# Experts of a two-layer decoder: raw float32 weights held in the array in 64-column tiles, 88 slots of tokens moving

## The chip, the cores and the metric

The kernel runs on one core of one Trainium2 chip. The metric is the device time of one execution in microseconds. Times come from three timed runs and from one profiled execution; instruction times (start and length in us) are those of the profiled execution.

## The reference

512 tokens of 1024 features go through two residual layers. Layer 0 mixes tokens by an RWKV-7 recurrence and a stick-breaking attention, layer 1 by a gated linear recurrence; all of that stays as it is. Each layer ends in a mixture of 16 experts, of which every token uses two:

```python
def hier_moe(h, ...):               # h = rmsnorm(x, norm_ffn[layer]), 512 x 1024
    ...                             # dense_gate: 512 x 16, two entries of a row not zero
    for e in range(N_EXPERTS):
        hid = jax.nn.silu(hf @ exp_w_gate[e]) * (hf @ exp_w_up[e])
        y = y + dense_gate[:, e:e + 1] * (hid @ exp_w_down[e])
```

An expert has 1024 x 512 weights for gate, as many for up, and 512 x 1024 for down, 6 MB of float32; 16 experts in two layers are 192 MB that are read once.

## The kernel before

**Routing.** `route_tile` runs once per tile of 128 tokens when the mixer has finished that tile (X). POOL multiplies the tile by the norm's gain (L1159), ACT's queue stores it in DRAM as HD (L1160) and the tile itself as YD (L1161), TensorE computes the router's logits (L1174). `choose` and `route` find every token's two experts, its place among an expert's tokens and its gate. Each expert has 96 slots (SL). For an expert's slots, `slots` compares places with slot numbers on VectorE (`match`, L1225), multiplies the result with the tokens' rows, gates and 1/rms on TensorE (`rows_of`, L1291) and reduces them on VectorE (L1283), so that each slot has three values: row of its token, gate, 1/rms. POOL gathers the slots' rows from HD (L1295).

**An expert.** `across` turns the 96 x 1024 gathered rows feature-major by eight transposes (L1306) and splits them into two float32r parts, hi and lo, whose sum is the float32 value: ACT copies (L296), VectorE subtracts (L297). Weights are split in the same way by `chunk`, in twelve half-parts an expert, of which POOL subtracts three and VectorE nine. Tokens stand in the array (128 x 96), weights move 512 columns at a time, and three matmuls (hi hi, lo hi, hi lo) make one float32 product: 24 for gate, 24 for up (L1317 to L1319), 24 for down (L1344 to L1346). The results are token-major, 96 partitions. SiLU with 1/rms as its scale runs on ACT (L1323), VectorE multiplies with up (L1456), `turn` transposes the hidden values (L1330) and splits them. `down` of expert e - 1 comes after gate and up of expert e; its two halves leave PSUM on ACT and VectorE, times the gate, and POOL adds them to YD in DRAM (L1353). The last expert's rows are added on chip (L1496 to L1510), after X has been read back from YD (L1481).

**Weights.** SP's queue loads an expert in six parts of 1 MB (L1371), at most five under way at a time, into a ring of slots of 2048 columns each. Gate and up parts have four rows of 2 KB per partition, down parts two of 4 KB. In layer 0 16 parts are loaded ahead, in layer 1 17; from there on a part's load waits until a slot is free.

**Order.** A scheduler orders each engine's instructions. `behind` adds order constraints: splits of the first expert's weights come after its slots are known, and so on. The SBUF has two arenas, A of float32 and R of float32r (12288 columns), R holding the split parts during the experts, and a piece S that changes its type.

## Time and profile before

| | |
|---|---|
| three runs, median (lowest to highest) | 1262.41 us (1259.56 to 1267.37) |
| profiled execution, span | 1262.0 us |
| TensorE busy | 1186.4 us, 94% |
| VectorE busy | 1028.6 us, 82% |
| ACT busy | 797.2 us, 63% |
| POOL busy | 497.1 us, 39% |
| DMA moved | 279.67 MB |
| mean granted TensorE clock | 0.971 |

The span is that of the first to the last instruction of the profiled execution, and the profiled execution is one more than the three timed ones. The experts of layer 0 take from 419.67 to 714.4 us, those of layer 1 from 954.2 to 1249.5, together 590 us of the 1262. A line of a timeline has start, length, engine, source line, operation, output tile and input tile, shapes (partitions x elements) and a count; for a matmul `128*64 128x88` is stationary rows x columns, then the moving operand. Matmuls are pipelined, so one starts before the one ahead of it has ended; what a matmul costs is read from the distance of starts. A float32 matmul leaves two records.

### The profile page before, as it was taken

The page shows a single profiled execution, that of the slowest core. Times are in us where ns is not written, and L with a number is a line of the kernel's source. Part 1 is how long each engine was busy: PE and PEld are TensorE (multiplying, and loading weights), DVE is VectorE, ACT ScalarE, POOL GpSimd, SP SyncE. Part 2 cuts the span into 40 slices and gives each one's busy share as a digit, 9 for nine tenths or more (in the row PEclk, how much of TensorE's full clock was granted, in tenths as well). Part 3 has the DMA queues.
Part 4 walks back from the last instruction along what each step waited for, and adds up shares of the span by engine and source line. Part 5 has one row for each costly group of instructions (what it writes and reads, how often), then busy time and mean ns, then how long its engine had stood idle before and what let it go on. Part 6 is the DMA issues. An engine that isn't in the chain of part 4 may idle for free. (4 is left out here: it accounts for less than half of the span.)

```text
span 1262.0 us, 17252 instructions
## 1 busy us (share of the span) xinstructions
PE 1186.4 (94%) x6234; PEld 875.7 (69%) x6235; DVE 1028.6 (82%) x1290; ACT 797.2 (63%) x1059; POOL 497.1 (39%) x326
## 2 busy tenths in 40 slices
PE   6999998999998799999999899999978999999997
PEld 5767765877676577777776676677865777777764
DVE  5387899577775899999998665599658999999985
ACT  6534332387653588888888564575435888888882
POOL 8043200211012347666775301220123466767752
PEclk9999999899998799999999999999987999999998
DMA  6312221001876799999998622267587999999974
GB/s 167 84 50 67 67 67 34 27 18 49 291 266 238 247 333 366 362 365 358 357 361 275 162 61 73 61 199 248 192 294 237 329 365 362 364 356 354 366 242 147
DMA packets 153060, 279.67 MB, mean 222 GB/s; under 512 B 7366, under 2 KB 58247, under 8 KB 152967
## 3 DMA queue, kind: packets, MB, share of 16 engines
q1 hardware_dynamic: 142886, 248.64, 56.8%
q0 software_dynamic: 7776, 21.47, 7.7%
q10 hardware_dynamic: 2304, 8.39, 1.7%
q8 instruction: 51, 0.84, 0.3%
q14 instruction: 43, 0.34, 0.1%
HBM read 259.59 MB, written 23.07 MB: 224 GB/s over the span
## 5 line engine op out<-in xcount | busy, mean ns | idle before, releaser
L296 ACT ACTIVATE R<-A 128x1024 fp32r<-128x1024 f32 (+1 forms) x451 | 473.2, 1053 | 201.7 <-PE ps_pj L1318 68.3
L297 DVE TENSOR_TENSOR R<-A,R 128x1024 fp32r<-128x1024 f32 (+1 forms) x362 | 493.1, 1397 | 77.2 <-ACT R L296 72.9
L297 POOL TENSOR_TENSOR R<-A,R 128x1024 fp32r<-128x1024 f32 x89 | 258.1, 2900 | 221.6 <-ACT R L296 219.8
L1317 PE MATMUL ps_pj<-R 128*96 128x512 f32 x512 | 204.9, 400 | 0.0
L1318 PE MATMUL ps_pj<-R 128*96 128x512 f32 x512 | 202.9, 396 | 1.6 <-DVE R L297 1.6
L1319 PE MATMUL ps_pj<-R 128*96 128x512 f32 x512 | 203.9, 398 | 0.0
L324 PE MATMUL ps_pj<-R 128*128 128x512 f32 x296 | 121.1, 409 | 9.9 <-DVE A L709 9.2
L326 PE MATMUL ps_pj<-R 128*128 128x512 f32 x296 | 119.3, 403 | 3.5 <-DVE R L297 3.5
L325 PE MATMUL ps_pj<-R 128*128 128x512 f32 x296 | 121.4, 410 | 0.0
L1318 PEld LDWEIGHTS ps_pj<-R 128*96 128x96 f32 x512 | 83.6, 163 | 37.7 <-DVE R L297 2.7
L1344 PE MATMUL ps_at<-R 128*96 128x512 f32 x256 | 103.8, 407 | 5.1 <-ACT R L296 1.9
L1319 PEld LDWEIGHTS ps_pj<-R 128*96 128x96 f32 x512 | 83.2, 163 | 36.0
L1317 PEld LDWEIGHTS ps_pj<-R 128*96 128x96 f32 x512 | 83.6, 163 | 34.2 <-ACT R L296 0.5
L1346 PE MATMUL ps_at<-R 128*96 128x512 f32 x256 | 101.6, 397 | 0.0
L1345 PE MATMUL ps_at<-R 128*96 128x512 f32 x256 | 101.5, 396 | 0.0
L324 PEld LDWEIGHTS ps_pj<-R 128*128 128x128 f32 x296 | 56.2, 190 | 27.6 <-DVE A L709 11.1
L1159 POOL TENSOR_TENSOR A<-A 128x1024 f32<-128x1024 f32 x8 | 20.9, 2623 | 135.3 <-DVE A L858 87.5
L326 PEld LDWEIGHTS ps_pj<-R 128*128 128x128 f32 x296 | 56.4, 191 | 20.7 <-DVE R L297 5.6
L1353 POOL DMA_INDIRECT YD<-A x30 | 67.3, 2245 | 4.8 <-issue 2.3
L325 PEld LDWEIGHTS ps_pj<-R 128*128 128x128 f32 x296 | 56.2, 190 | 15.3 <-issue 4.5
L1225 DVE TENSOR_TENSOR A<-A 128x384 bf16<-128x384 f32 (+2 forms) x34 | 61.8, 1818 | 0.0
L1295 POOL DMA_INDIRECT A<-HD,A x32 | 40.6, 1268 | 47.4 <-DVE A L1256 16.9
(440 smaller groups left out, 2067.7 us busy)
## 6 DMA issues: line engine op xcount, KB each, us to landing
A<-in_exp_w_up_dram SPq DMA_DIRECT2D x61, 1024.0 KB
A<-in_exp_w_down_dram SPq DMA_DIRECT2D x61, 1024.0 KB
A<-in_exp_w_gate_dram SPq DMA_DIRECT2D x59, 1024.0 KB
A<-in_w_in_even_dram SPq DMA_DIRECT2D x27, 512.0 KB
A<-in_w_in_odd_dram SPq DMA_DIRECT2D x20, 512.0 KB
S<-in_exp_w_gate_dram SPq DMA_DIRECT2D x5, 1024.0 KB
A<-in_w_out_odd_dram SPq DMA_DIRECT2D x10, 512.0 KB
A<-in_x_dram SPq DMA_DIRECT2D x8, 512.0 KB
```

Source lines behind the costliest of these rows:

```text
L296: a = self.nc.scalar.activation(hi, src, AF.Copy)
L297: return a, (eng or self.nc.vector).tensor_tensor(lo, src, hi.bitcast(F32), OP.subtract)
L324: nc.tensor.matmul(p[0:n], hi[:, k], Hh[:, k], start=k == 0, stop=False)
L325: nc.tensor.matmul(p[0:n], hi[:, k], Hl[:, k], start=False, stop=False)
L326: nc.tensor.matmul(p[0:n], lo[:, k], Hh[:, k], start=False, stop=k == KD - 1)
L1317: self.nc.tensor.matmul(b, xh[:, k], hi, start=k == 0, stop=False)
L1318: self.nc.tensor.matmul(b, xl[:, k], hi, start=False, stop=False)
L1319: self.nc.tensor.matmul(b, xh[:, k], lo, start=False, stop=k == KD - 1)
L1344: nc.tensor.matmul(yb[n], hh[:, k], hi[:, cs], start=k == 0, stop=False)
L1345: nc.tensor.matmul(yb[n], hl[:, k], hi[:, cs], start=False, stop=False)
L1346: nc.tensor.matmul(yb[n], hh[:, k], lo[:, cs], start=False, stop=k == 3)
L1353: self.nc.gpsimd.indirect_dma_start(out=self.YD[l][:, :], out_offset=bass.IndirectOffsetOnAxis(ap=ix[0:SL], axis=0), in_=y.rearrange("p a ...
```

## The change

**Weights aren't split.** The raw float32 weights are the stationary operand, in tiles of 128 rows and 64 columns, and tokens move (88 columns). `product` issues for one tile of 128 features eight matmuls for gate or up and sixteen for down; two neighbouring ones go to the left and right half of the array and write partitions 0 to 63 and 64 to 127 of one bank. An expert has 192 such matmuls instead of 72, with float32 products. Results are feature-major, so that the hidden values need no `turn`; the output of down does: `leave` copies it out of PSUM (ACT one half, VectorE the other), `back` transposes it (eight transposes of 128 x 128 to 88 x 128) and scales it by the gate. `down` runs in its own expert, after the next expert's `across`; `back` comes after the next expert's gate.

**88 slots** in place of 96. HD holds normed rows: `route_tile` computes 1/rms first, ACT multiplies by it, POOL by the gain while it reorders the features (reading with a stride of eight), into one buffer `hn`. 1/rms leaves the slots, which have two values.

**Loads.** Gate and up are laid out with features p*8 + c*4 + k, so that a part is one row of 8 KB per partition. R becomes float32 during the experts and holds six more weight slots; one old slot goes. 21 parts are loaded ahead in layer 0. The order constraints of `behind` go.

```diff
-SL = 96
-POOL = ((1, 1), (3, 1), (5, 1))
+SL = 88
...
     def route_tile(self, t):
+        r = self.rstd(t, self.ss)
         h = self.scr.next()
-        nc.gpsimd.tensor_tensor(h.f(), self.X.f(NT, D)[:, t], self.gn.f(), OP.mult)
+        nc.scalar.activation(h.f(), self.X.f(NT, D)[:, t], AF.Copy, scale=r)
+        n = self.hn.next()
+        turned = lambda a: a.rearrange("p (q k) -> p k q", k=KD)
+        nc.gpsimd.tensor_tensor(n.f(KD, 128), turned(h.f()), turned(self.gn.f()), OP.mult)
+        h = n
...
+    def leave(self, g, out, p):
+        pv = p[:, 0:4 * SL].rearrange("p (k t) -> p k t", k=4)
+        if g:
+            self.nc.vector.tensor_copy(out, pv)
+        else:
+            self.nc.scalar.activation(out, pv, AF.Copy)
+
+    def product(self, banks, raw, x, k, last):
+        for b, p in enumerate(banks):
+            pv = p[:, 0:4 * SL].rearrange("p (j n) -> p j n", j=4)
+            for j in range(4):
+                for s in range(2):
+                    q, c = slice(s * 64, s * 64 + 64), (b * 4 + j) * 128 + s * 64
+                    self.nc.tensor.matmul(pv[q, j], raw[:, c:c + 64], x, start=k == 0 and j == 0, stop=last, skip_group_check=True)
+
+    def half(self, w, x, chunk):
+        b = self.bank("pj")
+        for c in range(2):
+            raw = chunk(w * 2 + c)
+            for j in range(4):
+                k = c * 4 + j
+                self.product([b], raw[:, j], x[:, k], k, k == KD - 1)
+        return b[:, 0:4 * SL].rearrange("p (j n) -> p j n", j=4)
...
+    def back(self, yt, y=None, g=None):
+        nc = self.nc
+        yb = [self.bank("rw")[0:SL] for _ in range(2)]
+        for n in range(2):
+            for j in range(4):
+                nc.tensor.transpose(yb[n][:, j * 128:j * 128 + 128], yt[:, n * 4 + j], self.ident)
+        if y is None:
+            return yb
+        nc.scalar.activation(y[:, 0], yb[0], AF.Copy, scale=g)
+        nc.vector.tensor_scalar(y[:, 1], yb[1], g, None, OP.mult)
...
-            src = I["exp_w_gate" if i < 2 else "exp_w_up"][l].rearrange("e (c k p) n -> (e c) p k n", c=2, p=128)
-            return src, e * 2 + i % 2, (4, 512)
+            src = I["exp_w_gate" if i < 2 else "exp_w_up"][l].rearrange("e (p c k) n -> e c p (k n)", c=2, p=128)
+            return src[:, i % 2], (4, 512)
...
+        rr.drop(self.rat, RCOLS)
+        self.rat = ar.take(self.swap("R", F32), RCOLS)
         self.prefetch(l, 5, False)
         self.prefetch(l, 1, False, XB[0:1])
         if l:
             self.prefetch(l, 1, False, [self.more])
         self.prefetch(l, 1, False, XB[1:2])
+        self.prefetch(l, 6, False, [Buf(ar, self.rat.at + i * 2048, 2048) for i in range(6)])
         self.route(l)
...
-        self.prefetch(l, 1, False)
...
+        for e in range(NE):
             part = lambda i, e=e: self.chunk(l, e, i)
+            h = hr.next().f(4, SL)
+            self.front(h, self.half(0, x, part))
+            if e:
+                rest(e - 1)
             if e < NE - 2:
                 self.slots(e + 2)
                 fetch(e + 2)
-            if e:
-                h = self.turn(prev[0], hb)
...
+            b = self.half(1, x, part)
+            nc.vector.tensor_tensor(h, b, h, OP.mult)
+            if e < NE - 1:
+                x = turned(e + 1)
+                self.down(h, yv, part)
```

On TensorE, in the middle of layer 0's experts of the kernel before, the rows around one expert's first half of the next matmuls: the end of a `rows_of` (L1291), the transposes of the hidden values (L1330), the first three of the up matmuls.

```order
L1291 LDWEIGHTS A
L1291 MATMUL ps_o<-A 96x9
L1330 MATMUL ps_rw<-A 128x96 x4
L1317 MATMUL ps_pj<-R 96x512
L1318 MATMUL ps_pj<-R 96x512
L1319 MATMUL ps_pj<-R 96x512
```

The same place in the changed kernel, one expert's whole round: `across` (L1304), `rows_of` (L1289), down (L1324 into ps_at), the next expert's gate (into ps_pj), `back` (L1356), up.

```order
L1304 MATMUL ps_rw<-A 128x88 x8
L1289 LDWEIGHTS A
L1289 MATMUL ps_o<-A 88x6
L1324 MATMUL ps_at<-A 64x88 x64
L1324 MATMUL ps_pj<-A 64x88 x64
L1356 MATMUL ps_rw<-A 88x128 x8
L1324 MATMUL ps_pj<-A 64x88 x64
```

The triples of split parts are gone, tiled and whole-array matmuls take turns, and eight transposes of the output stand between gate and up.

On ACT, where the routing of layer 0 ends, before: the store of the last tile of HD (L1160) comes before the last tile's sum of squares (L286) and the Exps of the gates (L1246).

```order
L1172 ACTIVATE A<-ps_rw 128x512
L1161 DMA YD_66<-A 128x1024
L1160 DMA HD<-A 128x1024
L286 ACTIVATE A<-A 128x1024
L287 ACTIVATE A<-A 128x1
L288 ACTIVATE A<-A 128x1
L296 ACTIVATE R<-S 128x1024 x2
L1246 ACTIVATE A<-A 128x16
L1246 ACTIVATE A<-A 128x64
```

The same place in the changed kernel: scaled copy (L1159), two Exps (L1244), then the last store of HD (L1164).

```order
L1176 ACTIVATE A<-ps_rw 128x512
L287 ACTIVATE A<-A 128x1
L1159 ACTIVATE A<-A 128x1024
L1244 ACTIVATE A<-A 128x16
L1244 ACTIVATE A<-A 128x64
L1164 DMA HD<-A 128x1024
L1244 ACTIVATE A<-A 128x4
L1314 ACTIVATE A<-ps_rw 128x352
L1337 ACT_TABLE_LOAD
```

The store has moved behind the sum of squares, the copy and two Exps, and the ACT half of the first `across` (L1314) follows soon after.

On VectorE, where the first expert of layer 0 begins, before: the second match (L1225), its idx (L1285), then splits of weights and of the first `across` (L297 from ps_rw).

```order
L1283 TENSOR_REDUCE A<-ps_o 96x3
L1267 TENSOR_REDUCE A<-A 128x1
L1225 TENSOR_TENSOR A<-A 128x384
L1269 CAST A<-A 128x17
L1285 TENSOR_SCALAR A<-A 96x1
L297 TENSOR_TENSOR R<-S,R 128x1024 x2
L297 TENSOR_TENSOR R<-ps_rw,R 128x384 x2
```

The same place in the changed kernel: the last two of eight matches (L1228) that stand between the routing and the evacuation of the first `across` (L1312).

```order
L1228 TENSOR_TENSOR A<-A 128x352
L1283 TENSOR_SCALAR A<-A 88x1
L1281 TENSOR_REDUCE A<-ps_o 88x2
L1228 TENSOR_TENSOR A<-A 128x352
L1283 TENSOR_SCALAR A<-A 88x1
L1312 COPY A<-ps_rw 128x352
L1281 TENSOR_REDUCE A<-ps_o 88x2
```

Slots of later experts are computed here that before were computed between the experts.

## Rows read from the trace of the kernel before

**Rows 1.** the page: its head and the engines' busy time (share, instructions)

```profile
span 1262.0 us, 17252 instructions
...
PE 1186.4 (94%) x6234; PEld 875.7 (69%) x6235; DVE 1028.6 (82%) x1290; ACT 797.2 (63%) x1059; POOL 497.1 (39%) x326
```

**Rows 2.** windows: us, busy by engine, granted clock, DMA share, GB/s

```profile
600.00:617.88 17.88, 17.88 (x90) 12.76 (x89) 17.88 (x18) 14.79 (x17) 13.25 (x6) 1.00 1.04 361
```

**Rows 3.** timeline of ACT, two consecutive experts: start, us, line

```profile
602.55 0.67 ACT L1323 ACTIVATE A<-ps_pj,A 96x512 f32<-96x512 f32 x1
...
620.42 0.67 ACT L1323 ACTIVATE A<-ps_pj,A 96x512 f32<-96x512 f32 x1
```

**Rows 4.** timeline of PE inside one expert of layer 0

```profile
607.65 0.82 PE L1306 MATMUL ps_rw<-A 96*128 96x96 f32 x8
608.26 0.45 PE L1344 MATMUL ps_at<-R 128*96 128x512 f32 x1
...
613.86 0.39 PE L1317 MATMUL ps_pj<-R 128*96 128x512 f32 x1
...
619.42 0.30 PE L1291 MATMUL ps_o<-A 128*96 128x9 bf16 x4
619.58 0.53 PE L1330 MATMUL ps_rw<-A 96*128 96x96 f32 x4
```

**Rows 5.** the page's costliest groups: the split of weights

```profile
L297 DVE TENSOR_TENSOR R<-A,R 128x1024 fp32r<-128x1024 f32 (+1 forms) x362 | 493.1, 1397 | 77.2 <-ACT R L296 72.9
```

**Rows 6.** timeline of PE in layer 0's attention: 64-column pairs

```profile
261.69 0.64 PE L630 MATMUL ps_rw<-A 128*64 128x64 f32 x16
262.26 0.66 PE L786 MATMUL ps_at<-A 128*128 128x128 f32 x4
262.85 0.34 PE L641 MATMUL ps_rw<-A 128*64 128x64 f32 x4
...
276.68 1.09 PE L804 MATMUL ps_o<-A 128*64 128x128 f32 x16
277.70 1.10 PE L621 MATMUL ps_rw<-A 128*128 128x64 f32 x8
```

**Rows 7.** windows: that stretch of attention

```profile
268.00:280.00 12.00, 11.64 (x108) 8.98 (x109) 9.74 (x17) 9.72 (x19) 0.00 (x0) 1.00 0.01 1
```

**Rows 8.** timeline of all engines where layer 0's experts begin

```profile
400.55 2.35 POOL L1159 TENSOR_TENSOR A<-A 128x1024 f32<-128x1024 f32 x1 [3.51 <-DVE A L1189]
...
402.92 0.33 ACTq L1160 DMA_DIRECT2D HD<-A  x1
...
405.97 0.91 SPq L1371 DMA_DIRECT2D A<-in_exp_w_down_dram  x2
...
409.83 0.26 ACT L1246 ACTIVATE A<-A 128x64 f32<-128x64 f32 x1 [0.85 <-DVE A L1244]
...
413.98 1.09 POOL L1295 DMA_INDIRECT A<-HD,A  x1 [8.48 <-DVE A L1256]
...
419.67 0.23 PEld L1317 LDWEIGHTS ps_pj<-R 128*96 128x96 f32 x1 [0.23 <-ACT R L296]
```

**Rows 9.** DMA: instruction queues; gathers with median us to landing

```profile
q8 instruction: 51, 0.84, 0.3%
q14 instruction: 43, 0.34, 0.1%
...
A<-HD,A POOLq DMA_INDIRECT x32, 7.6
```

**Rows 10.** timeline of PE at the end of layer 0's experts

```profile
703.32 0.40 PE L1319 MATMUL ps_pj<-R 128*96 128x512 f32 x1
...
707.42 0.71 PE L1344 MATMUL ps_at<-R 128*96 128x512 f32 x1 [1.66 <-PEq L1536]
...
714.16 0.40 PE L1346 MATMUL ps_at<-R 128*96 128x512 f32 x1
```

**Rows 11.** timeline of PE, small matmuls of layer 0

```profile
232.71 4.32 PE L548 MATMUL ps_rw<-A 32*32 32x32 f32 x128
```

More of the change, by code (lines that the diff above doesn't have):

```diff
@@ new lines, in half, with front, down @@
+        return b[:, 0:4 * SL].rearrange("p (j n) -> p j n", j=4)
+    def front(self, h, b):
+        self.silu = self.nc.scalar.activation(h, b, AF.Silu)
+    def down(self, h, yt, chunk):
+        yb = [self.bank("at") for _ in range(2)]
+        for c in range(2):
+            raw = chunk(4 + c)
+            for j in range(2):
+                k = c * 2 + j
+                self.product(yb, raw[:, j], h[:, k], k, k == 3)
+        for n in range(2):
+            self.leave(n, yt[:, n * 4:n * 4 + 4], yb[n])
@@ L1392, in chunk @@
     def chunk(self, l, e, i):
-        shape = self.weights(l, e, i)[2]
-        raw = self.ahead.pop((e, i)) if (e, i) in self.ahead else self.load(l, e, i)
-        parts = []
-        h = shape[0] // 2
-        for j in range(2):
-            b = self.sp.next()
-            hi, lo = b.r(h, shape[1]), b.r(h, shape[1], off=1024)
-            pool = e > 0 and (i, j) in POOL
-            a, v = self.split(hi, lo, raw[:, j * h:j * h + h], self.nc.gpsimd if pool else None)
-            self.lastlo = v
-            if e == 0:
-                self.behind(a, self.mile[0])
-                if not pool:
-                    self.behind(v, self.mile[1])
-            if e == NE - 2 and i == 5:
-                self.behind(a, self.hidden[0])
-                if not pool:
-                    self.behind(v, self.hidden[1])
-            parts += [(hi[:, n], lo[:, n]) for n in range(h)]
-        return parts
+        return self.ahead.pop((e, i)) if (e, i) in self.ahead else self.load(l, e, i)
     def moe(self, l):
@@ L1497, in moe @@
             nc.vector.scalar_tensor_tensor(yl[:, n], yb[n], g, yh[:, n].bitcast(F32), OP.mult, OP.subtract)
-        for b in (*self.wt.bufs, self.sp, xgr, hr, yr, self.idx, self.sg, self.lastt):
-            if b not in XB and b is not more:
+        for b in (*self.wt.bufs, xgr, xtr, hr, yr, yt, self.idx, self.sg, self.lastt):
+            if b not in self.lent:
                 b.free()
@@ L1567, in overflow @@
-                    r = sg.f()[0:SL, 2:3]
-                    self.front(hd.f(p=(0, SL)), self.half(0, xh, xl, chunk), r)
-                    b = self.half(1, xh, xl, chunk)
-                    nc.vector.scalar_tensor_tensor(hd.f(p=(0, SL)), b, r, hd.f(p=(0, SL)), OP.mult, OP.mult)
-                    self.down(self.turn(hd.f(p=(0, SL)), hb), y, chunk, sg.f()[0:SL, 1:2])
+                        src, shape = self.weights(l, i)
+                        src = src[bass.ds(e, 1)].rearrange("a p k -> p (a k)" if i < 4 else "a p k n -> p (a k) n")
@@ L1572, in overflow @@
+                        nc.sync.dma_start(wt.f(2048) if i < 4 else wt.f(*shape), src)
+                        return wt.f(*shape)
+                    h = hd.f(4, SL)
+                    self.front(h, self.half(0, xv, chunk))
+                    nc.vector.tensor_tensor(h, self.half(1, xv, chunk), h, OP.mult)
+                    self.down(h, yt, chunk)
+                    self.back(yt, y, sg.f()[0:SL, 1:2])
                     self.scatter(l, y, ix.i(1))
```

206 lines of the change are left out of this document (71 added, 135 removed).

## Prediction

> **What bounds the kernel now.** I read the page's busy times first, then the clock and busy time of one steady stretch, then the lines of one expert. TensorE is busy 1186 of 1262 us [rows 1], so only its work or its gaps can give anything back. The 16 experts of a layer follow each other with a period of 17.88 us: two SiLUs of neighbouring experts start at 602.55 and 620.42 [rows 3]. In a stretch of that length TensorE is busy for all 17.88 us at the full granted clock, and so is VectorE; the DMA engines' share is 1.04 at 361 GB/s [rows 2]. Three resources are full at once, so a change that relieves one of them alone gives nothing. This one takes work from all three: VectorE's 362 subtractions of 1.4 us, 493 us in all [rows 5], go from the experts; TensorE's 72 matmuls an expert are replaced; and six more slots let the weights lead by more. What decides is TensorE's price of an expert, since VectorE is left with a handful of copies of some 0.5 us.
>
> Before, an expert costs TensorE 72 x 0.233 us (24 down matmuls stand between 608.26 and 613.86), 0.61 for the eight `across` transposes, 0.16 for the four `rows_of` and, by `across`, 0.31 for four `turn` transposes [rows 4]: 16.8 + 1.1 = 17.9, the period.
>
> **The new expert on TensorE.** It has 64 + 64 + 64 matmuls in column pairs, each matmul leaving two records in the trace, so 192 pairs of records. Layer 0's attention has pairs of the same form, float32, 128 rows, 64 stationary columns, halves of the array in turn, at the full clock [rows 7]. L804 moves 128 columns: 16 records in 1.09 us, the last 0.27 long, are 0.82/7.5 = 109 ns a pair. L630 moves 64: 16 records in 0.64, the last 0.22, are 0.42/7.5 = 56 ns a pair [rows 6]. For 88 moving columns the price lies between; linear in the columns it is 56 + 24/64 x 53 = 76 ns. 192 x 76 = 14.6 us. To it come:
> - `across`, eight transposes as before: 0.6 [rows 4].
> - `back`, eight transposes of 128 columns, the counterpart of the four old ones: by `across` 0.61 x 128/96 = 0.8, by L786, four in 0.59 with a change of shape on either side, 1.2 [rows 4, 6]; I take 0.9.
> - `rows_of`: 0.16.
> - changes between whole-array and half-array matmuls, four or five an expert. L786 between two tiled groups takes 0.59, where four at 109 ns would take 0.44 [rows 6]: 0.15 for two changes. With the first matmuls of each stream I take 0.5, and 0.25 for VectorE's product of gate and up, which `down` waits for and which the next `across` mostly covers.
>
> Sum 17.0 us, against 17.88. The loop for tokens beyond an expert's slots stays empty: counted from the reference's inputs, no expert has more than 84 tokens, against 88 slots. Bounds: 16.4 without the last two entries, 17.8 with a pair at 79 ns, `back` at 1.2 and 0.65 for changes.
>
> [...]
>
> **The start of a layer's experts.** Before, the first expert's first weights load at 419.67. Three things move there, all towards later. First, the store of the last HD tile goes at 402.92 now, right behind POOL's product that ends at 402.90. In the new order of ACT it stands behind two Exps that wait for VectorE, the second at 409.83 [rows 8], and the gather, which reads HD, cannot run before the store has landed. POOL's product with strided reading (2.35 us now; its new price is not in the trace, 2.3 to 6 us) hides in that wait of 7 us, as does ACT's new scaled copy ahead of it, a pass over the same tile. Second, six more loads are issued around 406, where now two are [rows 8], so store and gather share the queues. Gathers take 7.6 us in the median of all 32 [rows 9], most of them beside weight loads; the first one now takes from 413.98 to about 418. Third, VectorE has eight matches ahead of the first evacuation of `across` instead of two. At about a microsecond for match, `rows_of` and reduction this ends near 423, beside the slower gather, not after it. Between no delay (all of it hidden) and 10 us (store at 410, 3.5 to land, a gather of 7.6, 2 for transposes and evacuation: 423; plus the matches not hidden) I take 5: start at 424.7.
>
> **The end.** The last expert: gate and up 2 x 4.9, `back` of expert 14 0.9; then the gap of today, from the last up matmul at 703.32 to the first down matmul at 707.42 [rows 10], 4.1 with the old `turn` in it, so 3.3; `down` 4.9 and 1.5 for slow first matmuls behind the gap (today's `down` takes 6.98 us between 707.42 and its end at 714.4 [rows 10], against 5.6 in the steady stretch [rows 4]); then 1.5 for `leave` and `back`, which didn't exist. Sum 21.9.
>
> **The sum.** A layer's experts end at 424.7 + 15 x 17.0 + 21.9 = 701.6 instead of 714.4: 12.8 us less, in two layers 25.6. 1262.0 - 25.6 = 1236.4; span and median of the runs (1262.41) are the same within the spread, so 1237 us. The weights' DMA adds nothing to it. An expert moves 6 x 1.05 MB of weights and some 0.7 MB of gather and scatter; at today's 361 GB/s [rows 2] that is 19.4 us, more than 17.0. The lead pays for it: 21 parts are under way at the start, the other 75 need 75 x 3.23 = 242 us from 427 on, so the last one is in by 669 or a little later, and it is needed near 694.
>
> **Rivals.**
> (a) *Weight loads serialize: slower.* If the two halves cannot load side by side, a pair costs what a whole-array load costs: L621, 128 columns stationary and 64 moving, leaves 8 records in 1.10 us, 0.82/7 = 118 ns [rows 6]. 192 x 118 = 22.7 and 2.4 for the rest make an expert of 25 us, 128 us more a layer than forecast: some 1493. It decides as soon as a pair costs over 81 ns, from where an expert takes 17.9. L630's 56 ns speaks against it; for it, that its streams are only eight matmuls long and that L641's four records take 0.26 us, two pairs with two changes. [...] Chance 0.05.
> (b) *Instructions arrive too slowly: slower.* The new stream has four instructions in 76 ns (two weight loads, two matmuls), 850 an expert with the transposes. The two instruction queues fetched 1.18 MB for 17252 instructions, 68 bytes each, and q8 in packets of 0.84/51 MB = 16 KB, some 240 instructions, at 0.3% of 16 engines' span, 1.2 us a packet [rows 1, 9]; an expert needs 3.5 of them. If each fetch stood in the way, 3.5 x 1.2 = 4.2 us an expert, 134 in all: some 1371. Against it: L548's 128 matmuls with 128 loads run in 4.32 us [rows 11], a faster stream. But that one is a single packet long. [...] Chance 0.07.
> (c) *The DMA binds.* If the last parts come late: the lead of 25 us is gone when a load takes 3.23 + 25/75 = 3.56 us, 10% over today, which rows of 8 KB don't suggest. At 15% over, 3.71 x 75 = 278 from 427 ends at 705, 11 late a layer: 1259, no change. Chance 0.05.
> (d) *The start eats it.* A delay of 10 us a layer and an expert of 17.5 us: 1237 + 10 + 15 = 1262, no change. What speaks for it: three delays in one chain, and none of them priced by a row alone. Chance 0.15.
> (e) *Cheaper than thought.* Expert of 16.5, no delay at the start: 1237 - 16 - 10 = 1211. Chance 0.08; the forecast itself, 1216 to 1250, has 0.60.
>
> **Chances.** Runs of this kernel tell about 1% from no change, 12.6 us. The forecast and (e) are faster but for the upper edge; (c) and (d) are within 1%; (a), (b) and a fifth of (d) are slower. Faster 0.68, same 0.17, slower 0.15. The range goes from 1211, the end of (e), to 1270, the side of (d): it leaves out (a), (b) and little else.
>
> **What would show it.** In the changed profile: SiLUs 17.0 us apart instead of 17.88; groups of 64-column matmuls at 38 ns from record to record; VectorE's share in such a stretch under a third; DMA share still near 1. The first expert's matmul some 5 us later than 419.67, with the gather's landing as what PE waits for. Wrong it is if SiLUs stand over 17.9 apart, with idle PE that nothing releases (b) or a wait for weights (c), or if the records stand 55 ns or more apart (a).

## The result, and the profile after

The changed kernel is slower: 1318.1 us, median of five runs (1306.9 to 1318.9), against 1264.1 (1259.6 to 1267.4) of the kernel before, a ratio of 1.041 with a 95% interval of 1.037 to 1.045. The forecast was 1237, its range ended at 1270. The profiled execution is the shortest of the five (1306.9, span 1304.8); the others have spans of 1316 to 1317 at a mean granted clock of 0.952 to 0.957 against its 0.963. All stage times below are those of the profiled execution; the further 11 us of the others were not traced to a stage.

The head of the page of the changed kernel, with the instruction queue's row (packets, MB, share of 16 engines' span), answers to [rows 1, 9]:

```profile
span 1304.8 us, 36099 instructions
...
PE 1164.9 (89%) x16346; PEld 1006.3 (77%) x16347; DVE 561.4 (43%) x954; ACT 399.7 (31%) x651; POOL 219.2 (17%) x236
...
q8 instruction: 132, 2.16, 0.7%
```

TensorE was busy 94% of the span and is now busy 89%: the change has opened idle time on the engine that it was to relieve. VectorE fell from 1029 to 561 us as foreseen. The program has twice the instructions, and q8 fetches 132 packets instead of 51.

Where the time came from, in us, by the timelines of both kernels (the forecast's column by its own sum; a layer's experts go from the first matmul with their weights to the end of the last expert's `down`, which before the change is 714.56 in layer 0 [rows 10], not 714.4):

| stage | before | forecast | after |
|---|---|---|---|
| up to the experts of layer 0 | 419.7 | 424.7 | 427.6 |
| experts of layer 0 | 294.9 | 276.9 | 308.5 |
| from there to the experts of layer 1 | 239.6 | 244.8 | 247.0 |
| experts of layer 1 | 295.4 | 277.5 | 309.7 |
| the rest | 12.4 | 12.5 | 12.0 |
| span | 1262.0 | 1236.4 | 1304.8 |

Of the 68 us between forecast and profile 64 stand in the two rows of the experts. The steady stretch of layer 0, in the columns of [rows 2]:

```profile
core 0: us, PE busy (x) PEld busy (x) DVE busy (x) ACT busy (x) POOL busy (x), PEclk, DMA share, GB/s
470.00:660.00 190.00, 167.59 (x3878) 160.66 (x3879) 26.24 (x57) 19.23 (x39) 25.69 (x19) 0.99 1.01 352
```

The clock is full, the DMA engines are as full as before, and TensorE lies idle for 22 of 190 us. The SiLUs of neighbouring experts (timeline of ACT; [rows 3] before):

```profile
568.14 0.46 ACT L1337 ACTIVATE A<-ps_pj 128x352 f32<-128x352 f32 x1 [5.86 <-PE ps_pj L1324]
586.10 0.47 ACT L1337 ACTIVATE A<-ps_pj 128x352 f32<-128x352 f32 x1 [5.60 <-PE ps_pj L1324]
606.54 0.46 ACT L1337 ACTIVATE A<-ps_pj 128x352 f32<-128x352 f32 x1 [7.45 <-PE ps_pj L1324]
...
699.52 0.46 ACT L1337 ACTIVATE A<-ps_pj 128x352 f32<-128x352 f32 x1 [4.94 <-PE ps_pj L1324]
716.15 0.47 ACT L1337 ACTIVATE A<-ps_pj 128x352 f32<-128x352 f32 x1 [4.94 <-PE ps_pj L1324]
```

17.96 and 20.44 us apart in the middle of the layer, 16.63 at its end, where the loads are over. From the second SiLU to the last it takes 265.5 us in layer 0 and 269.1 in layer 1; 14 undisturbed experts of 16.65 would be 233.1. The difference, 32 and 36 us, is what has to be explained. TensorE's timeline in the stretch of the first two SiLUs (in brackets the idle time ahead and what ended it):

```profile
564.62 1.05 PE L1324 MATMUL ps_pj<-A,S 128*64 128x88 f32 x21 [0.66 <-issue]
565.44 2.66 PE L1324 MATMUL ps_pj<-A 128*64 128x88 f32 x64
568.03 1.07 PE L1356 MATMUL ps_rw<-A 128*88 128x128 f32 x8
568.94 0.17 PE L1289 MATMUL ps_o<-A 128*88 128x6 bf16 x1
569.04 1.50 PE L1324 MATMUL ps_pj<-A 128*64 128x88 f32 x33
570.91 3.86 PE L1324 MATMUL ps_pj<-A 128*64 128x88 f32 x95 [0.37 <-issue]
574.70 0.83 PE L1304 MATMUL ps_rw<-A 88*128 88x88 f32 x8
575.37 0.17 PE L1289 MATMUL ps_o<-A 128*88 128x6 bf16 x1
575.47 5.07 PE L1324 MATMUL ps_at<-A 128*64 128x88 f32 x128
580.37 1.07 PE L1324 MATMUL ps_pj<-A 128*64 128x88 f32 x23
581.83 0.37 PE L1324 MATMUL ps_pj<-A 128*64 128x88 f32 x4 [0.39 <-issue]
```

First the price: 128 records, 64 pairs (a float32 matmul on a half of the array leaves two records, and a pair of records is what the forecast prices), go from 575.47 to 580.37, 76.6 ns a pair; the forecast had 76. Then the gaps. Nothing that the trace shows releases them ("issue"). From the gap at 564.62 to that at 570.91 there are 127 matmul records, and each has its weight load: 254 instructions. From there to the gap at 581.83 there are 255, so 510 instructions. Counted on all records of the layer, neighbouring gaps stand 256, 512, 768 or 1024 instructions apart, to within two records, and a packet of the instruction queue is 2.16 MB / 132 = 16 KB, 64 bytes for each of 256 instructions. The trace also has the times of q8's packets: each of the 24 gaps of layer 0 between its second and last SiLU ends 1.23 to 1.60 us after the end of a packet. By this TensorE waits at the border of a packet for that packet, at some borders and not at others: 45 packets of q8 start in that stretch, and 24 gaps stand there.

The waits of TensorE and of SP's queue in the experts of layer 0 (us in total, times, longest; one more gap, of 0.9 us, is put down to a SiLU on ACT, and it too stands at such a border):

```profile
PE ps_pj L1324 <- issue: 16.5, 16, 2.9
PE ps_at L1324 <- issue: 5.4, 6, 1.9
```

```profile
SPq L1383 <- PE ps_pj L1324: 158.2, 51, 20.3
SPq L1383 <- PE ps_at L1324: 67.4, 24, 4.2
```

TensorE never waits for weights. For the experts' parts SP waits for slots that TensorE has not given back, never for a landing: the loads keep their lead of 21 parts to the end, the last is issued at 669.7, and the lead is never spent.

Theories at this point. **A**: instruction packets share the DMA engines with the weights (in 500:600 q1, which moves the most, takes 84.5% of the 16 engines' time, q0 15.4, q8 1.2), and beside full traffic the next packet comes too late for a stream that uses one up in 4.9 us. **B**: fetching has this limit by itself (the forecast's rival (b)). **C**: the gaps don't come from the fetch at all, but from the tile stream itself or from what it reads.

### The profile page after: what moved, and what is told of

Read it like the earlier page. It is cut to its first block, busy times and chain, and to the rows that moved or that the text cites. A ratio compares the mean times of both kernels' runs of the same rounds, so it can differ in the third digit from the quotient of the medians.

```text
span 1304.8 us, 36099 instructions
## 1 busy us (share of the span) xinstructions
PE 1164.9 (89%) x16346; PEld 1006.3 (77%) x16347; DVE 561.4 (43%) x954; ACT 399.7 (31%) x651; POOL 219.2 (17%) x236
## 3 DMA queue, kind: packets, MB, share of 16 engines
q8 instruction: 132, 2.16, 0.7%
## 5 line engine op out<-in xcount | busy, mean ns | idle before, releaser
L1324 PE MATMUL ps_pj<-A 128*64 128x88 f32 x5696 | 236.2, 242 | 25.3 <-issue 25.2
L1324 PEld LDWEIGHTS ps_pj<-A 128*64 128x64 f32 x5696 | 226.0, 138 | 31.7 <-issue 30.5
L1324 PE MATMUL ps_at<-A 128*64 128x88 f32 x2944 | 122.0, 243 | 18.7 <-PEq L1517 12.7
L1324 PEld LDWEIGHTS ps_at<-A 128*64 128x64 f32 x2944 | 117.1, 139 | 21.1 <-issue 19.9
L295 ACT ACTIVATE R<-A 128x1024 fp32r<-128x1024 f32 (+1 forms) x89 | 91.0, 1028 | 111.0 <-PE ps_pj L324 63.4
L296 DVE TENSOR_TENSOR R<-A,R 128x1024 fp32r<-128x1024 f32 (+1 forms) x85 | 102.9, 1212 | 47.4 <-ACT R L295 44.1
L1363 POOL DMA_INDIRECT YD<-A x30 | 47.5, 1584 | 448.7 <-DVE A L1360 194.5
L1360 DVE TENSOR_SCALAR A<-ps_rw,A 88x512 f32<-88x512 f32 x30 | 22.4, 747 | 199.1 <-PE ps_rw L1356 187.5
L1324 PE MATMUL ps_pj<-A,R 128*64 128x88 f32 x2048 | 86.0, 242 | 9.3 <-issue 9.3
L1324 PEld LDWEIGHTS ps_pj<-A,R 128*64 128x64 f32 x2048 | 82.2, 139 | 11.3 <-issue 11.3
L1312 DVE COPY A<-ps_at 128x352 f32<-128x352 f32 x32 | 16.8, 524 | 160.8 <-PE ps_at L1324 160.8
L1314 ACT ACTIVATE A<-ps_rw 128x352 f32<-128x352 f32 x32 | 14.9, 464 | 202.4 <-PE ps_rw L1304 202.4
L324 PEld LDWEIGHTS ps_pj<-R 128*128 128x128 f32 x296 | 56.1, 190 | 15.4 <-issue 4.7
L1314 ACT ACTIVATE A<-ps_at 128x352 f32<-128x352 f32 x32 | 14.9, 464 | 157.8 <-PE ps_at L1324 157.8
```

The source lines that it names most:

```text
L295: a = self.nc.scalar.activation(hi, src, AF.Copy)
L296: return a, (eng or self.nc.vector).tensor_tensor(lo, src, hi.bitcast(F32), OP.subtract)
L324: nc.tensor.matmul(p[0:n], hi[:, k], Hl[:, k], start=False, stop=False)
L1312: self.nc.vector.tensor_copy(out, pv)
L1314: self.nc.scalar.activation(out, pv, AF.Copy)
L1324: self.nc.tensor.matmul(pv[q, j], raw[:, c:c + 64], x, start=k == 0 and j == 0, stop=last, skip_group_check=True)
```

## The experiments

The time of each is set against the kernel before on the same chip (1260.3 to 1268.8 over all experiments). "2nd to last" is the time from the second SiLU of a layer to its last, gaps are idle times of TensorE over 0.15 us in that stretch, with their sum; two values are layers 0 and 1. Where no interval is given, a kernel ran once; five executions of the changed kernel lie 12 us apart, so that smaller differences in time between such runs say nothing, and what is read from them is read from their traces. Diffs are against the changed kernel, but for the last three, each of which is against the run ahead of it; `...` stands for lines left out.

**Without traffic (e1).**

```diff
+        if e >= 4:
+            self.loads.append(self.loads[-1])
+            return b.f(*shape)
```

> Leaves out the weight loads of experts 4 to 15 in both layers (these experts multiply with whatever is in the slots); all instructions of TensorE stay. Theory A (TensorE's instructions are fetched by the same DMA engines as the weights, and the fetch comes late while the engines are full): from about expert 4 on no gap that nothing releases, SiLUs 16.7 us apart as in the last three experts of a layer, experts of layer 0 some 30 us shorter than the 308.5 us of the changed kernel, whole kernel about 1245. Rival B (a block of instructions takes longer to fetch than to run, whatever else the engines do): the gaps stay, 24 in layer 0, and the time stays at about 1300. Rival C (gaps are waits for weights under another name): they vanish too, but only where a load was left out and PE had overtaken it; the loads that remain would show it.

Measured: 1243.6 us (before 1261.5). 2nd to last 233.4 and 234.2, gaps none and one of 0.5; a layer's experts take 275.6 and 274.1. Windows and SiLUs:

```profile
470.00:660.00 190.00, 190.00 (x4591) 185.93 (x4588) 31.02 (x69) 23.27 (x45) 31.05 (x23) 1.00 0.22 42
```

```profile
567.41 0.46 ACT L1337 ACTIVATE A<-ps_pj 128x352 f32<-128x352 f32 x1 [4.94 <-PE ps_pj L1324]
584.14 0.46 ACT L1337 ACTIVATE A<-ps_pj 128x352 f32<-128x352 f32 x1 [4.94 <-PE ps_pj L1324]
```

The same stream fetched by the same queue runs at 16.7 us an expert without a gap. B falls, and of C the tile stream itself. This run alone doesn't exclude that the loads disturb what the stream reads; against it speaks that every gap stands at the border of a packet and ends shortly after the packet has come. The experts' rows of the forecast, 276.9 and 277.5, come close here, in part by luck: 15 periods of 16.65 us are 5 us less than 15 of 17.0, and the rest of a layer takes 25.9 and 24.4 us where the sum had 21.9.

**Half and two thirds of the traffic.** The same edit with `e >= 4 and i in (1, 3, 5)`, and with `i in (2, 5)`.

> Leaves out three of the six weight parts of experts 4 to 15 (these multiply with what is in the slots), so that the DMA engines are about half busy. Theory A, a late fetch while engines are full: at half load hardly a gap, under 3 us in a layer against 23.5, SiLUs 16.7 to 17 us apart. If any weight traffic at all delays a fetch enough: gaps stay at a third or more of the changed kernel's, 8 us or more.

> The same with four of six parts loaded, DMA engines about 0.75 busy. A gives gaps of 2 to 10 us a layer here; if the lateness sets in only when the engines are full, under 2 us as with half the loads; if it goes with the traffic, about two thirds of 23.5, 16 us.

| run | us | DMA share, GB/s in 510:660 | gaps: number, sum | 2nd to last |
|---|---|---|---|---|
| e1, no late loads | 1243.6 | 0.22, 41 | 0; 1 of 0.5 | 233.4; 234.2 |
| half | 1258.9 | 0.70, 205 | 7, 4.4; 8, 5.6 | 241.0; 241.4 |
| two thirds | 1261.0 | 0.85, 263 | 9, 6.9; 9, 9.1 | 243.2; 245.1 |
| all (the changed kernel) | 1306.9 | 1.00, 352 | 24, 23.5; 23, 26.0 | 265.5; 269.1 |

Half of the loads give 4.4 and 5.6 us of gaps, between the two outcomes that were expected; two thirds fall into the 2 to 10 of theory A. The loss against 233.1 grows with the traffic: 8, 10 and 32 us in layer 0, steepest towards the full share. The gaps in the table sum to less than the loss, since an idle time begins at the modelled end of the last matmul (242 ns after its start, where the next would start 38 ns after it: 24 x 0.2 = 5 us) and gaps under 0.15 us are left out.

**How the traffic is made.** Fewer loads under way, smaller rows, more spread in time:

```diff
-FLY = 5
+FLY = 2
```

> At most two weight loads under way in place of five. Theory A in the form that the fetch waits in line behind queued weight packets: gaps shrink by more than half, SiLUs 17 to 18 us apart, kernel 1265 to 1280, unless two loads can't keep the DMA engines busy. A in the form that the fetch merely gets its share of a full engine: gaps stay as they are while the engines are full. If two loads move less than some 330 GB/s, weights arrive late in the second half of a layer, and TensorE waits for DMA there: 1310 or more. Rival B: no change.

```diff
...
-            src = I["exp_w_gate" if i < 2 else "exp_w_up"][l].rearrange("e (p c k) n -> e c p (k n)", c=2, p=128)
+            src = I["exp_w_gate" if i < 2 else "exp_w_up"][l].rearrange("e (c k p) n -> e c p k n", c=2, p=128)
...
```

> Gate and up weights in rows of 2 KB as before the change, and POOL's product without the stride. If 8 KB packets are what a fetch waits behind, gaps go down by half or more and the kernel to 1270 or less. If the packet size doesn't matter: gaps as before, experts of layer 0 within 3 us of 308.5 us, kernel about 1300. POOL's product goes from 3.9 back to 2.4 us; that is hidden unless the start comes earlier by the same 1.4 us.

```diff
...
+            self.used.append(self.mm)
...
+        n = len(self.loads)
+        if n >= self.n0 > 0:
+            self.tc.add_manual_dep(d.ins, self.used[(n - self.n0) * (88 - 0) // (95 - self.n0)].ins.name, mybir.DependencyInfo(
...
```

> Each load from the 22nd on also waits until TensorE has used a given part, so that the lead of 21 parts shrinks evenly to 7 by the end of a layer; nothing else changes. In the changed kernel loads run as soon as a slot is free and the lead is never spent. If the gaps come from engines that are full for most of a layer and idle at its end, spreading the loads (some 320 GB/s in place of 350) takes gaps down to 10 to 16 us and the experts of layer 0 from 308.5 to 295 to 302 us, kernel 1285 to 1300. If the fetch is late at any such load, no change within 3 us a layer; if parts come late, TensorE waits for DMA near the end and the layer gets longer.

Measured: 1314.1, 1313.8 and 1311.5 us. With two loads under way the traffic is 311 GB/s and there are 16 gaps a layer, 23.3 and 22.9 us; of the latter 6.5 are waits for weights, which come too slowly then. With rows of 2 KB the gaps are 29.7 and 26.0; with loads bound to TensorE's progress 22.8 and 22.2, at 304 to 321 GB/s throughout layer 0. None of the three came to the shorter times that were expected if its edit met the cause. Neither the depth of the queue nor the length of a row nor bursts are the cause: at any of these rates, 304 to 344 GB/s, packets come late.

**The other way round: nearly the same traffic, a slower stream (e11).** 128 slots make a pair longer and leave the number of instructions as it is.

```diff
-SL = 88
+SL = 128
...
-        self.prefetch(l, 5, False)
+        self.prefetch(l, 4, False)
```

> 128 slots in place of 88 (and one weight slot fewer, for room): the same instructions, each pair of matmuls at the 109 ns of the attention's 128-column pairs, so that 256 instructions last 7.0 us instead of 4.9. A fetch that is up to 2 us late then still comes in time. Theory A: gaps nearly gone (under 4 us a layer against 23.5), an expert 192 x 0.109 + 2.0 = 22.9 us, all of them alike, kernel 1304.8 + 2 x 14 x (22.9 - 19.0) + some 15 = about 1430. If the gaps had to do with the amount of weight traffic alone or with waits for it, they would stay near 20 us a layer and an expert take 24.5, kernel 1475.

Measured: 1458.4 us, no gap in layer 0 and one of 0.2 in layer 1, a SiLU every 23.3 to 23.4 us between the second and the last but one. Windows and a piece of TensorE's timeline:

```profile
510.00:660.00 150.00, 150.00 (x2594) 146.41 (x2590) 22.47 (x43) 16.02 (x26) 17.47 (x13) 1.00 0.94 301
```

```profile
568.20 7.21 PE L1324 MATMUL ps_at<-A,R 128*64 128x128 f32 x128
575.24 7.16 PE L1324 MATMUL ps_pj<-A,R 128*64 128x128 f32 x128
582.33 1.09 PE L1356 MATMUL ps_rw<-A 128*128 128x128 f32 x8
```

Here 256 instructions last 7.0 us, and at 301 GB/s none is late; in the changed kernel they last 4.9 us, and at 304 to 321 GB/s (the paced loads) 23 us a layer are lost. Traffic and the rate of the stream are both needed. A smaller step of the same kind:

```diff
-SL = 88
+SL = 96
```

> 96 slots in place of 88, as many instructions, each pair of matmuls 9% longer (76.6 to about 83 ns, 1.2 us an expert). Theory A: the stream asks for a block every 5.3 us in place of 4.9, so the fetch has more time; the gaps shrink by what the matmuls grow, SiLUs in the full part stay at some 19 us, and only the undisturbed experts grow from 16.65 to 17.9. Kernel 1300 to 1315. Rival D (TensorE is bound by its matmuls and gaps come on top): all experts 1.2 us longer, 38 us in two layers, kernel 1340.

Measured: 1312.3 us; an undisturbed expert takes 18.0 instead of 16.65, the gaps fall to 12.8 and 9.9. Eight per cent more work on TensorE cost nothing that shows beside the changed kernel's 1306.9 to 1318.9: the gaps took it up.

**Start and end.** The six early loads put behind the first gather; the loop for tokens beyond the slots left out, which for these inputs never runs; the way to HD as in the kernel before (product in place, rows of 2 KB).

```diff
...
+        if self.first is not None:
+            self.tc.add_manual_dep(d.ins, self.first.ins.name, mybir.DependencyInfo(
...
-        self.prefetch(l, 6, False, [Buf(ar, self.rat.at + i * 2048, 2048) for i in range(6)])
...
-        fetch(0)
+        self.first = fetch(0)
+        self.prefetch(l, 6, False, [Buf(ar, self.rat.at + i * 2048, 2048) for i in range(6)])
```

> The six new loads of a layer wait until the first expert's rows are gathered. If the store of HD (8.5 us to landing) and the first gather (7 us) are slow because those loads share the queues: the first expert of layer 0 starts near 421 in place of 427.6, that of layer 1 as much earlier, and the kernel is 10 to 14 us shorter, unless the later loads are then missed by TensorE. If order on ACT and POOL alone makes the delay, the start stays within 2 us of 427.6.

```diff
-        self.overflow(l, xgr.bufs[0], xtr.bufs[0], hr.bufs[0], yv, yr.bufs[1], XB[0])
+        for b in (self.ext, self.pm, self.sl):
+            b.free()
```

> Leaves out the loop for tokens beyond an expert's 88 slots, which is empty with these inputs, with its branch on each engine. If the 7.3 and 5.3 us ahead of the last down are that branch on TensorE (its taken jump lasted 4.0 and 5.6 us in the changed kernel, 0.3 us before the change): both gaps shrink to under 1.5 us, the kernel by some 10 us. If they are the wait for VectorE's product of gate and up, they stay.

```diff
-        self.scr, self.hn, self.ht = Ring(ar, 2, D, lo), Ring(ar, 1, D, lo), Ring(ar, 2, D, lo)
+        self.scr, self.ht = Ring(ar, 3, D, lo), Ring(ar, 2, D, lo)
...
-        n = self.hn.next()
-        turned = lambda a: a.rearrange("p (q k) -> p k q", k=KD)
-        nc.gpsimd.tensor_tensor(n.f(KD, 128), turned(h.f()), turned(self.gn.f()), OP.mult)
-        h = n
+        nc.gpsimd.tensor_tensor(h.f(), h.f(), self.gn.f(), OP.mult)
...
```

> The changed kernel with a shorter path to HD: rows of 2 KB for gate and up, so that POOL's product has no stride, and it works in place in a ring of three buffers (no single buffer that waits for the store before). If this path makes the late start: first expert of layer 0 at 421 to 424 in place of 427.6. If the six loads beside the store and the gather make it, as the run with those loads behind the gather says: 426 to 428. In both cases the kernel stays at 1300 to 1318, since an earlier start was eaten before.

The next one joins the paced loads and the loads behind the gather.

> The same, and the six new loads wait for the first gather. The start at 419.6 of that experiment was eaten by longer experts (319.7 us), as the loads then had to be made up for at once. With the loads spread the 8 us should stay in part: kernel 6 to 14 us under the paced one. If the stage simply ends when the DMA has moved its bytes, the end stays where the paced kernel has it.

| run | us | first tile matmul, layer 0 | after the last store of HD | its experts | gaps |
|---|---|---|---|---|---|
| the changed kernel | 1306.9 | 427.63 | 19.9 | 308.5 | 23.5; 26.0 |
| six loads behind the gather | 1307.0 | 419.64 | 12.0 | 319.7 | 28.0; 26.6 |
| HD as before, 2 KB rows | 1313.4 | 421.75 | 15.3 | 324.2 | 28.7; 25.8 |
| 2 KB rows, no stride (above) | 1313.8 | 427.37 | 16.6 | 318.3 | 29.7; 26.0 |
| paced (above) | 1311.5 | 432.53 | 19.7 | 309.6 | 22.8; 22.2 |
| paced and behind the gather | 1310.1 | 424.33 | 11.4 | 316.1 | 26.2; 25.5 |
| no loop | 1309.8 | 427.20 | 20.2 | 303.9 | 25.6; 27.1 |

Both paced runs and that with 2 KB rows and no stride are some 5 us late before any of HD is stored, so the start is better read from the last store. That lateness arises in layer 0's mixer: in 225:250 TensorE's granted clock is 0.66 to 0.73 in these three and 0.86 to 0.93 in the other four.

Six loads behind the gather and the old way to HD start the experts 8 and 6 us earlier, and the experts take 11 and 16 us longer; of the 16 some 10 come with rows of 2 KB, by the fourth row. With six loads later SP waits for landings too (36.5 us in 16 waits for `down`'s parts alone). With paced loads the start comes 8 us earlier as well, and the experts take 6.5 us longer. Without the loop the gap ahead of the last `down` falls from 7.34 to 0.70 us and from 5.33 to 0.70, and the experts are 4.6 and 3.9 us shorter; but TensorE then waits 3.6 us for X from YD, and from the end of layer 0's experts to the start of layer 1's it takes 258.1 us in place of 247.0, so that the time stays within the spread of the changed kernel. In none of the four did the local effect reach the total. For the earlier starts a reason that fits is that they move more work into the stretch with traffic, where packets set TensorE's pace; no run tests that by itself.

**Fewer instructions, versions that might beat both.** Gate and up stay on tiles; `down` goes back to split weights moving 512 columns, its matmuls between the groups of gate and up, one expert later. That is 34 instructions per us on TensorE (2035 in 60 us, first row of the windows below) where the tile stream has 48 (9179 in 190, e1's window).

```diff
...
+    def low(self, yb, h, w, c, j):
...
+            self.nc.tensor.matmul(yb[n], hh[:, k], hi[:, cs], start=k == 0, stop=False)
+            self.nc.tensor.matmul(yb[n], hl[:, k], hi[:, cs], start=False, stop=False)
+            self.nc.tensor.matmul(yb[n], hh[:, k], lo[:, cs], start=False, stop=k == 3)
...
+            self.piece(g, 0, x, part(0))
+            if e:
+                w = self.halves(self.chunk(l, e - 1, 4))
+                self.low(yb, hh, w, 0, 0)
+            self.piece(g, 1, x, part(1))
...
```

> Gate and up as in the change (raw float32 weights as 64-column tiles), down as before the change (weights split on ACT and VectorE, moving 512 columns, one expert late), its matmuls in four groups of six between the pieces of gate and up; R stays float32r, so 15 weight slots in layer 0. An expert costs TensorE 128 pairs x 76.6 ns + 24 x 0.233 + 0.6 + 0.2 + some 0.6 for changes = 16.8 us with 600 instructions in place of 850, so that 256 of them last 7 us. Theory A: no gaps, SiLUs 16.8 us apart, experts of a layer some 285 us instead of 308.5 (before: 294.7), kernel 1235 to 1250, faster than both. If weight traffic alone slows TensorE: gaps of 15 us or more a layer and 1262 or more. A third outcome: 15 slots are too few, TensorE waits for weights towards the end of a layer, 1250 to 1262.

Measured: 1275.4 us, ratio to before 1.009 (1.005 to 1.012), longer than the two outcomes without gaps. Up to the tenth SiLU an expert takes 17.3 us, almost without a gap, at 357 GB/s. Then SiLUs stand 17 to 23 us apart, and what is late are the weights; ACT's waits in 480:680:

```profile
ACT R L295 <- DMA A<-in_exp_w_down_dram: 55.7, 10, 10.1
```

The experts of a layer take 293.1 and 292.2 us in this run, 2 to 3 less than in the kernel before. What makes it slower stands ahead of them: layer 0's start at 428.3 in place of 419.7 (some 5 us of it are the mixer's clock, 0.73 in 225:250 against 0.86), and 250.3 us between the two layers' experts in place of 239.6.

Three more runs built on it: one with HD's path as above and with the expert before last's `down` finished early, ahead of the second half of the last expert's gate; one that adds a weight slot (16 instead of 15) to that; one that goes back from rows of 2 KB to 8 KB in it.

```diff
...
+            if e == NE - 1:
+                self.low(yb, hh, w, 0, 1)
+                w = self.halves(self.chunk(l, e - 1, 5))
+                self.low(yb, hh, w, 1, 0)
+                self.low(yb, hh, w, 1, 1)
...
```

> Down as before the change (the run with no gaps), with the shorter path to HD, and in the last expert the down of expert 14 ahead of the second half of gate, so that its rows are added and X is read back earlier. Start of layer 0 near 421 in place of 428.3, of layer 1 as much earlier, X back 6 us earlier: 1274.8 - 14 - 4 = about 1255. If the loads, not the start, set the end of a layer (15 slots), the kernel stays at 1265 to 1275.

```diff
...
+        self.rat, q = self.swap("R", None)
+        q = ar.take(q, 2048)
+        self.prefetch(l, 1, False, [q])
...
```

> The same with one more weight slot in what R has left. Experts 10 to 14 took 17.2 to 22.7 us with 15 slots, waiting for weights; with 16 slots 3 us less of that. 3 us a layer under the kernel without it, 1245 to 1255; if it is under 1262 by more than the interval, this version beats both.

```diff
+        nc.scalar.activation(h.f(KD, 128), turned(self.X.f(NT, D)[:, t]), AF.Copy, scale=r)
+        nc.gpsimd.tensor_tensor(h.f(KD, 128), h.f(KD, 128), turned(self.gn.f()), OP.mult)
...
```

> As the run with one slot more, but gate and up in rows of 8 KB; ACT does the reordering of HD's features while it scales, POOL multiplies in place. If a layer is bound by its loads and the wider rows load faster: second to last SiLU 246 to 251 us in place of 260, kernel 1279 - 2 x 11 = 1250 to 1262, at or under the kernel before (1262 to 1265). If the row width doesn't matter to the loads, 1275 to 1280, and the difference of the earlier runs came from elsewhere.

Measured, in this order: 1283.0; 1279.8, ratio 1.011 (1.008 to 1.015); 1275.7, ratio 1.009 (1.005 to 1.012). None came in under the kernel before. The first two missed what was expected; the third has the time of its second outcome. In the second the experts start early (420.7 in layer 0, then 239.3 us after the end of layer 0's), but they take 302.0 and 306.5 us. Rows of 8 KB shorten the time from second to last SiLU from 260.0 and 261.4 to 253.7 and 253.5 us, so the width of rows counts in this kernel; but layer 0 starts at 427.3 again. The windows of the last one:

```profile
500.00:560.00 60.00, 60.00 (x1018) 49.20 (x1017) 27.28 (x37) 21.36 (x28) 12.46 (x7) 1.00 1.02 354
560.00:620.00 60.00, 60.00 (x1026) 49.64 (x1025) 25.76 (x37) 20.42 (x27) 11.85 (x7) 1.00 1.03 356
620.00:680.00 60.00, 54.75 (x882) 44.64 (x880) 22.73 (x34) 17.74 (x26) 10.93 (x6) 0.97 1.02 355
```

At 2035 instructions in 60 us, 7.5 us per packet, TensorE has no gap beside 354 GB/s. But an expert of 17.3 us eats weights faster than they arrive: 6.3 MB and 0.7 of gather and scatter at 355 GB/s are 19.7 us. When the 16 slots' lead is gone, TensorE waits for loads. No version was found that beats the kernel before. That one too outruns its loads a little (17.88 us at 361 GB/s are 6.5 MB an expert), but its lead of 16 parts lasts to the end of the layer: TensorE has no wait for weights there.

## Why the prediction was wrong, step by step

**The step that failed** is the sentence "The weights' DMA adds nothing to it", and with it the dismissal of rival (b). I reckoned the traffic only against the weights' own arrival; there the lead was more than enough, as SP's waits show. What the traffic did to the instruction fetch I did not reckon. The term that stands at nothing in the sum came to 32 and 36 us in the two layers. The runs show it: no gap at 42 GB/s with the same stream (e1), none to speak of at 301 GB/s with a stream that uses a packet in 7.0 us (e11), 23 to 26 us of gaps a layer where a fast stream and full traffic meet.

**Rival (b)** had the right resource, with 0.07. My evidence against it, L548's 128 matmuls in 4.32 us [rows 11], was too short and in the wrong place: it is one packet, as I wrote, and it runs far from the weight loads, beside a DMA share of 0.15 and 48 GB/s (232.70:237.03 of the kernel before). It could not show what the second packet does beside 350 GB/s. My price, 3.5 fetches of 1.2 us standing fully in the way, was not the mechanism either: a packet's own transfer takes 1.08 us in the mean of q8's records in layer 0's experts, and 1.06 to 1.13 without traffic. What is late is its start. From the first instruction of a block, the 256 instructions of one packet, to the start of the next packet the median is 3.6 us in the changed kernel and 2.1 with half the traffic, and a block's first instruction comes 1.2 us or more after its packet's end. 3.6 + 1.1 + 1.2 = 5.9, more than the 4.9 us that a block of tile pairs lasts and less than 7.0; with half the traffic it is 4.4. These are medians, and with half the traffic single packets still come late (7 gaps). That both sides of 4.9 come out as measured supports the reading, but what holds a packet's start back was not tried.

**TensorE's price of an expert** was right: 76.6 ns a pair against 76, and 16.65 to 16.7 us an expert against 17.0. Rival (a), serialized weight loads at 118 ns a pair, was rightly set aside. The expert of 16.5 us in (e) was an estimate that no run shows; they showed 16.65 to 16.7 where no gap stood. Two bounds of the sum for an expert don't add up as written: without the last two entries it is 16.3, and the upper one is 18.0; neither changes the outcome.

**The period** came out near what the loads need anyway: with its gaps TensorE took about 19 us an expert in the mean (265.5/14), near the 19.7 of the loads' pace. So the lead of 21 parts, which was to pay for the difference, never came into use. Rival (c), the binding DMA, did not happen, since nothing waited for a landing.

**The start** was forecast 5 us late and came 8.0 and 7.4 late. The chain in layer 0, in the timelines:

```profile
401.64 3.81 POOL L1162 TENSOR_TENSOR A<-A 128x1024 f32<-128x1024 f32 x1 [6.15 <-ACT A L1159]
...
407.71 0.33 ACTq L1164 DMA_DIRECT2D HD<-A  x1
...
426.07 1.41 PE L1304 MATMUL ps_rw<-A 88*128 88x88 f32 x8 [8.95 <-DMA A<-HD,A]
...
427.63 4.94 PE L1324 MATMUL ps_pj<-A,S 128*64 128x88 f32 x64
```

```profile
416.26 1.83 POOL L1430 MEMSET A<- 88x1024 f32 x2 [10.81 <-DMA HD<-A]
418.31 1.16 POOL L1293 DMA_INDIRECT A<-HD,A  x1 [0.22 <-POOL A L1430]
```

The strided product takes 3.8 us (2.35 before, [rows 8]), inside the bounds given. The store left at 407.71, earlier than the 410 of the far case, but it took 8.5 us until the memset behind it could run, beside weight loads that SP had issued at 406 and 407; I had 3.5 us for it, which no row gave. And POOL's memset waits for that landing, since the gathered rows reuse the store's buffer, a wait that I had not named. Two runs each take a part of this away: the six loads behind the gather, and HD as before, with three buffers:

```profile
407.62 0.33 ACTq L1164 DMA_DIRECT2D HD<-A  x1
...
410.38 1.97 POOL L1433 MEMSET A<- 88x1024 f32 x2 [4.85 <-DMA HD<-A]
```

```profile
398.19 1.83 POOL L1427 MEMSET A<- 88x1024 f32 x2 [2.90 <-issue]
...
406.44 0.33 ACTq L1161 DMA_DIRECT2D HD<-A  x1
...
411.02 1.16 POOL L1290 DMA_INDIRECT A<-HD,A  x1 [7.29 <-DVE A L1260]
```

Without the six loads the same store lets the memset run 2.8 us after it left, and the experts start 12.0 us after the store; in the other run the memset stands ahead of the last store, and they start 15.3 us after it; in the changed kernel it is 19.9. So it is store and gather beside the six loads that cost, with the memset between them; the path to HD alone does not make it. When the store leaves decides what it meets: in layer 0 the first of the loads was issued 1.6 us ahead of it, and it took 8.5 us; in layer 1 the first was issued 0.2 us behind it (965.24 and 965.01), and it took 3.5. The other runs with the six loads there bear this out: 7.9 to 8.9 us with the first load 0.3 us or more ahead, 3.5 to 3.9 with it 0.2 us or more behind. In layer 1 10.8 us then pass from the first gather's issue at 970.73 to the transposes at 981.54.

**The end.** I took the old gap without its `turn`, 3.3 us. It became 7.34 and 5.33. TensorE's timeline, and the branch into the loop that is passed over, in the changed kernel and before (ns min/median/max):

```profile
717.04 5.08 PE L1324 MATMUL ps_pj<-A 128*64 128x88 f32 x128
729.45 6.67 PE L1324 MATMUL ps_at<-A 128*64 128x88 f32 x128 [7.34 <-PEq L1517]
```

```profile
L1517 PEldq COMPARE_BRANCH  x2: 3972/4798/5623, 723.3 to 1282.0; - x2
```

```profile
L1536 PEldq COMPARE_BRANCH  x2: 318/336/353, 706.8 to 1241.6; - x2
```

The same jump over an empty loop costs 4.0 to 5.6 us instead of 0.3. The loop's body has grown with the expert's 192 matmuls. q8's records have packets that start inside the two jumps of the changed kernel (724.81, 725.98 and 1283.52), and none inside layer 0's jump before, where they start at 694.32 and 708.60; what makes the jump longer was not shown. The run with `down` as before has some 600 instructions an expert in place of 850, and its jumps still take 3.4 and 3.8 us; a body as short as the old one was not tried with tiles. Taking the loop out brought the gap down to 0.70, which shows the place, and left the total alone.

**The signs** that I named for being wrong were the right ones to watch: SiLUs over 17.9 us apart with idle TensorE that nothing releases was listed for (b), and it is what the profile shows.

## What to carry to other kernels

Before a stream of few long instructions is replaced by one of many short ones, divide the 256 instructions that a packet had here by its instructions per microsecond and look for a stretch of the trace that runs at that pace over several packets beside the traffic it will meet; here 4.9 us a packet was too fast beside 300 GB/s and more, some 5.3 (4.9 x 18.0/16.65, the 96 slots) still lost 10 to 13 us a layer, and 7.0 to 7.5 us was not too fast. A resource that seems paid for by a lead can still cost through what else shares it, here 32 and 36 us a layer in late packets. And where a stage is paced by such a limit, an earlier start, a removed gap or a few per cent of engine work may change nothing, as here: take the limit away first.

## What the runs showed that I had not expected

- Idle time of TensorE at multiples of 256 instructions, to within two records, put down to "issue", and gone at 42 GB/s.
- A fetch whose own transfer hardly changes (1.08 us) while its start comes 1.5 us later at full traffic than at half.
- A taken branch on TensorE that goes from 0.3 us to between 4.0 and 5.6 where the code that it passes over has grown.
- POOL's product of 128 x 1024 with a stride of eight in its operands: 3.86 us in the mean of eight, against 2.62 before.
